# Masked block of the attention probabilities left out, and a later finish of the differential norms

## Chip, cores and metric

The kernel runs on one core of one Trainium2 chip. The metric is the device time of one execution in microseconds (us), the median of three runs. Engines are named as in the profile: PE is TensorE's matmul, PEld its weight load, DVE is VectorE, ACT is ScalarE, POOL is GpSimd, SP is SyncE.

## What is computed

The reference is a decoder of four layers on 512 tokens of width 1024, all in float32. The first block has a layer with a short convolution and a layer with sparse attention (compressed, selected and window branches of 12 heads); both also attend to a memory. The second block has a layer of multi-head latent attention (8 heads) and one of differential attention (8 heads); each layer ends in a squared-ReLU MLP. What the change touches is causal attention:

```python
def _causal_probs(q_blk, k, q_start, scale):
    s = jnp.einsum('bqhd,bkhd->bhqk', q_blk, k).astype(jnp.float32) * scale
    s = jnp.where(k_idx[None, :] <= q_idx[:, None], s, -jnp.inf)
    return jax.nn.softmax(s, axis=-1)
...
        p1 = _causal_probs(q_blk[..., 0, :], k1, start, scale)
        p2 = _causal_probs(q_blk[..., 1, :], k2, start, scale)
        a = p1 - lam * p2
        return jnp.einsum('bhqk,bkhd->bqhd', a.astype(v.dtype), v)
    o = _rmsnorm(o, subln) * (1.0 - lambda_init)
```

A query never sees a later key, so of any two tiles of 128 queries and the two tiles of 128 keys at the same place, the block (earlier queries, later keys) of the probabilities is zero.

## The kernel before

Nearly every product is kept exact by a split: a float32 matrix is written as a high part (dtype float32r, `FR`) and a low part, `split` (L91 to L99, ACT writes the high part, DVE the low one), and three products high x high, high x low, low x high are added up in PSUM (`mm`, L91, so that all these matmuls stand under line L91 and are told apart by tile names). The instruction streams of the engines are put in order when the program is built: every instruction has a priority, its place in the code, and a planned time at which it is ready; each engine's queue is then run strictly in order on the chip. A tile gets a buffer when one of its tag is free. PSUM has eight banks, two each of the tags S, T, F and O.

Attention works in units, one for a head (in the sparse layer: a head and a branch) and a half of the queries, that is two query tiles. `pipeline` (L388) runs three stages of successive units a step or more apart:
- `first`: scores (tile `sp`, two bank S tiles), `soft_half` (L402: DVE subtracts the maximum, ACT takes the exponential into tile `z`), `scale_half` (L432, L435: POOL multiplies `z` by the reciprocal of the row sum). In differential attention `first` makes two score maps, and DVE adds them at L1436.
- `turned`: `probs_T` (L437) transposes the blocks of `z` on TensorE (tile `pT`, L451) and splits them into `pth` and `ptl`, both from the pool of six pairs that the split weights (`wh`, `wl`) come from as well. The block that is masked is not transposed; it is filled with zeros by a DVE memset (L441) and a POOL memset (L442).
- `second`: the product with the values, `av` (three products for a key tile, tiles `lo` in latent and `do` in differential attention) or `av_stack` (two products, tile `no`), each 256 queries wide, into a bank of tag O (`bankB`).

There are 48 units in the sparse layer (6 pairs of heads x 2 heads x 2 halves x 2 branches), 16 in latent and 16 in differential attention, 80 in all. Memory attention uses `av_stack` too, without a mask.

In differential attention `second` (L1443) goes on: ACT squares the product (L1452), TensorE sums the squares over the partitions (`ones`), DVE and POOL make the reciprocal root (`var` L127, `rstd` L129). What is left is the closure `third` (L1457): TensorE turns the root into a row in the other half of the same bank (L1459), ACT copies it (L1460), DVE multiplies (L1461), and a split writes `oT`. `third` of a unit is put into the list `pend` and called in the `second` of the next unit, after that unit's product with the values.

Steps are filled up with dense work (`fills`): in differential attention the query, key and value layer of later heads (tile `df`, steps 0 to 11) and half of the output layer (tile `wo`, one unit of 12 matmuls in steps 10 to 17). The head's transposes of its keys (tile `dkT`) take a bank of tag O as well.

Of the kernel before, what the change touches and what calls it, by code (L numbers as in the profile page):

```python
# [32 lines left out]
def model_kernel(ctx: ExitStack, tc: tile.TileContext, I, out, tap=lambda *a: None, stop=0):  # L33
# [67 lines left out]
    # ------------------------------------------------------------ constants  # L101
# [30 lines left out]
    # ------------------------------------------------------------ weights  # L132
# [24 lines left out]
    # ------------------------------------------------------------ dense layers  # L157
    def dense_a(nK, lhs, weights, chunks, evac, tail=4, ntok=MT, late=None, ahead=3, hook=None):
        """Token-major layer: activations stationary, weights moving; late() brings the last token tile."""
        nch = len(chunks)  # L160
        dst = {}

        def alloc(t):
            if t in dst:
                return
            if nch == 2:
                if t == 0:
                    rot["S"] = rot["T"] = 0
                dst[t] = list(bankST("acc")) if t < 3 else [bankB("acc"), bankB("acc")]
            else:  # L170
                dst[t] = [bankT("acc") if t % 2 else bankS("acc")]

        W = {}

        def step(k, t, cs=range(nch)):
            alloc(t)
            wh, wl = W[k]
            lh, ll = lhs(k, t)
            for a, b, st, sp in ((lh, wh, k == 0, False), (lh, wl, False, False), (ll, wh, False, k == nK - 1)):
                for c in cs:  # L180
                    c0, c1 = chunks[c]
                    mm(dst[t][c][:, :c1 - c0], a, b[:, c0:c1], st, sp)

        head = max(0, nK - tail)
        k0 = 0
        if late is not None:
            k0 = min(ahead, nK)
            for k in range(k0):
                W[k] = weights(k)
            for t in range(ntok):  # L190
                if t == 2:
                    late()
                for k in range(k0):
                    step(k, t)
        for k in range(k0, head):
            W[k] = weights(k)
            for t in range(ntok):
                step(k, t)
        k0 = max(k0, head)
        for k in range(k0, nK):  # L200
            W[k] = weights(k)
        if hook:
            hook()
        for t in range(ntok):
            if nch == 2 and t == ntok - 1:
                for c in range(2):
                    for k in range(k0, nK):
                        step(k, t, (c,))
            else:
                for k in range(k0, nK):  # L210
                    step(k, t)
            evac(t, [dst[t][c][:, :c1 - c0] for c, (c0, c1) in enumerate(chunks)])

    def dense_b(xh, xl, nK, nU, weights, late, early):
        """Feature-major layer: units of 256 features; weights(u, k0) gives 4 k tiles.  With late(), the first
        two units take tokens 0-255 before it and 256-511 after it.  Yields the unit's PSUM tile; with early, the
        next unit's weights are asked for before that."""
# [41 lines left out]
    # ------------------------------------------------------------ norms and transposes  # L259
# [24 lines left out]
    def next_xT(norm):  # L284
        """norm(t, ps) -> token-major tile.  The last tile's transposes are left to the next layer (box["late"])."""
        box = {}

        def after(t, ps):
            if t == 0:
                box["xT"] = new_xT()  # L290
            if t > 0:
                to_xT(box["xT"], t - 1, box["src"])
            src = box["src"] = norm(t, ps)
            if t == MT - 1:
                box["late"] = lambda: to_xT(box["xT"], t, src, True)

        return after, box
# [33 lines left out]
    def dup_heads(src):  # L331
        """[P, t, (2 heads, 64)] -> [P, t, head, twice, 64]."""
        d = w4("dup").rearrange("p (t h r d) -> p t h r d", t=MT, h=2, r=2)
        for r in range(2):
            nc.gpsimd.tensor_scalar(d[:, :, :, r, :], src.rearrange("p t (h d) -> p t h d", h=2), 1.0, 1.0,
                                    op0=OP.mult, op1=OP.mult)
        return d
# [6 lines left out]
    # ------------------------------------------------------------ parameter columns  # L344
# [28 lines left out]
    def stack(dst0, dst1, T, key):  # L373
        """T [(head0 d; head1 d), cols] -> [high; low] of each head, gains applied."""
# [12 lines left out]
    # ------------------------------------------------------------ attention pieces  # L387
    def pipeline(units, lags, extras=None, fills=None, started=0):  # L388
        """Step s issues stage i of unit s - lags[i]; extras, fills: {step: closures issued before, after}."""
# [12 lines left out]
    def soft_half(half, scores, bias, scale):  # L402
        """Query tiles 2*half, 2*half+1: exp(s - max) in z[:, b, :], reciprocal row sums."""
# [20 lines left out]
    def falling(v):  # L424
        """The columns of v in falling order."""
        n = v.shape[-1]
        return bass.AP(tensor=v.tensor, offset=v.offset + n - 1, ap=[list(v.ap[0]), [-1, n]])
# [9 lines left out]
    def probs_T(half, z):  # L437
        """-> key tile -> [keys, 256 queries], high and low parts.  The masked block leads the last pair of tiles."""
        h, l = pair("pt")
        o = half * 512  # L440
        nc.vector.memset(h[:, o:o + P].bitcast(FT), 0.0)  # L441
        nc.gpsimd.memset(l[:, o:o + P].bitcast(FT), 0.0)  # L442
        for a in range(half + 1):
            T = bankT("pT")
            skip = P if a == half else 0
            for c in range(2):
                kt = 2 * a + (1 - c if skip else c)
                for b in range(2):
                    c0 = c * 256 + b * P
                    if c0 >= skip:  # L450
                        nc.tensor.transpose(T[:, c0:c0 + P], z[:, b, kt * P:(kt + 1) * P], ident)  # L451
            cs = slice(a * 512 + skip, (a + 1) * 512)
            split(h[:, cs], l[:, cs], T[:, skip:])

        def tile_of(kt):
            k = (kt ^ 1 if kt // 2 == half else kt) * 256
            return h[:, k:k + 256], l[:, k:k + 256]

        return tile_of

    def av(o, vs, pt, nkt, first=True, last=True):
        for kt in range(nkt):
            vh, vl = vs(kt)
            ph, pl = pt(kt)
            mm(o, vh, ph, first and kt == 0, False)
            mm(o, vh, pl, False, False)
            mm(o, vl, ph, False, last and kt == nkt - 1)

    def av_stack(o, vs, pt, nkt, first=True, last=True):
        """vs(kt): [keys, (high | low) of 64 columns]; rows 0-63 and 64-127 of o add up to the product."""  # L470
        for kt in range(nkt):
            ph, pl = pt(kt)
            mm(o, vs(kt), ph, first and kt == 0, False)
            mm(o, vs(kt), pl, False, last and kt == nkt - 1)
# [7 lines left out]
    # ------------------------------------------------------------ memory attention  # L482
# [7 lines left out]
    def mem_kv(L, mT):  # L490
        """Emits the layer's key/value product; the returned closure finishes the keys."""
# [31 lines left out]
    def mem_attention(L, qm, ks, v, oT):  # L523
# [10 lines left out]
        for i in range(0, MT, 2):  # L534
            for a in range(2):
# [25 lines left out]
                def second(i=i, a=a, st=st):  # L561
# [10 lines left out]
                    for b in range(2):  # L572
                        ob = bankB("mo")[:, :256]
                        av_stack(ob, lambda kt: v[:, kt, 2 * a + b].rearrange("p s d -> p (s d)"), lambda kt: (h[:, b, kt], l[:, b, kt]), 2)
# [9 lines left out]
    def wrounds(src, ld, c0, n, key=None):  # L584
        """Blocks of k tiles of n columns, row gains applied when key is given."""
# [27 lines left out]
    def w_out_part(src, base, oT, ks, alpha=None):  # L613
        """Units that add k tiles ks of the output layer to the residual ahead of w_out."""
# [57 lines left out]
    # ------------------------------------------------------------ rotary tables  # L672
# [38 lines left out]
    def rope(dst, src, t, nh, nf, key):  # L711
        """dst, src: [P, nh, head width]; rotates the first 2*nf columns."""
# [13 lines left out]
    # ============================================================ first block, layer 0  # L726
# [5 lines left out]
    # ---- relative bias functions of the second layer  # L732
# [110 lines left out]
    # ============================================================ first block, layer 1  # L843
    # ---- keys, values, queries, gates
# [30 lines left out]
    # ---- compressed keys and values  # L875
# [78 lines left out]
    # ---- compressed, selected and window branches  # L954
# [181 lines left out]
    # ============================================================ second block  # L1136
# [16 lines left out]
    # ---- multi-head latent attention  # L1153
# [49 lines left out]
    def rope_q(g4):  # L1203
        """Rotated query parts of heads 4*g4 .. 4*g4 + 3, token-major."""
# [106 lines left out]
    # ---- differential attention  # L1311
# [18 lines left out]
    def diff_w(n, half):  # L1330
        """Half of the weights of part n % 3 of round n // 3."""
# [3 lines left out]
    def diff_round(r, bank):  # L1335
        """Dense units of heads 2*r, 2*r + 1: rotated queries and keys, split values, all token-major."""
# [64 lines left out]
    for h in range(8):  # L1401
# [17 lines left out]
        for half in range(2):  # L1419
# [23 lines left out]
            def second(h=h, half=half, st=st, ph=ph):  # L1443
# [5 lines left out]
                while pend:  # L1449
                    pend.pop()()  # L1450
# [19 lines left out]
    pend.pop()()  # L1470
# [59 lines left out]
```

## Time and profile before

| what | value |
|---|---|
| median of 3 runs | 2418.26 us (2415.67 to 2418.78) |
| span of the profiled execution | 2418.3 us |
| PE busy | 2362.6 us, 98% of the span |
| PEld, DVE, ACT, POOL busy | 2032.3, 1223.3, 969.4, 273.6 us |
| chain that ended last | PE 89%, DVE 4%, ACT 3%, POOL 2%, issue 1%, DMA 1% |

The span of the profiled execution is, to its last digit, the median of the runs, so that microseconds of the trace can be taken off the median as they are. The three attention stages lie at about 676 to 876 us (sparse), 1275 to 1410 us (latent) and 1785 to 2037 us (differential). The duration of a matmul in the trace contains its latency; in a stream the next one starts earlier, and the distance between two starts is what a matmul costs.

### The profile page before, as it was taken

Reading aid. Unit: us, or ns where it says so; the run is one execution under the profiler, and the core shown is the slowest. Engines: PE = TensorE matmul, PEld = TensorE weight load, DVE = VectorE, ACT = ScalarE, POOL = GpSimd, SP = SyncE. Lnnn points to the kernel's source line nnn. Section 1 sums busy time; section 2 is a strip of 40 time slices with the busy share of each in tenths; the row PEclk is TensorE's granted clock in tenths of the full one; section 3 lists DMA queues with packets and bytes.
Section 4 is the critical chain, followed back from the end, with each engine's and each line's share of the span. In section 5 each row is a group of like instructions: output and inputs, shape, how many; then the busy total and the mean of one; then the engine's idle time right before and its main releaser. Section 6 shows DMA issues by size and latency. Waiting matters only on the chain.

```text
span 2418.3 us, 32335 instructions
## 1 busy us (share of the span) xinstructions
PE 2362.6 (98%) x12735; PEld 2032.3 (84%) x12735; DVE 1223.3 (51%) x2248; ACT 969.4 (40%) x1749; POOL 273.6 (11%) x458
## 2 busy tenths in 40 slices
PE   8999999999988999999999999999999999999998
PEld 7878888888877888888888888888889997888886
DVE  5564333336678873333347773333356667433334
ACT  4353332225468853332225543222235555323222
POOL 0220000000345520000001100000011222000000
PEclk9999999999999999999999999999999999999999
DMA  6223322224211133222221133322221112332222
GB/s 199 88 75 122 105 89 86 96 96 139 67 36 36 45 102 105 89 87 96 96 84 47 63 113 105 105 79 96 96 90 53 63 62 79 122 105 79 96 96 70
DMA packets 149538, 214.90 MB, mean 89 GB/s; under 512 B 12570, under 2 KB 119389, under 8 KB 149386
## 3 DMA queue, kind: packets, MB, share of 16 engines
q1 hardware_dynamic: 148718, 212.54, 27.5%
q8 instruction: 100, 1.64, 0.3%
q14 instruction: 52, 0.43, 0.1%
q10 hardware_dynamic: 668, 0.30, 0.0%
HBM read 210.68 MB, written 2.13 MB: 88 GB/s over the span
## 4 chain that ended last, share of the span: by engine, by line
PE 89%; DVE 4%; ACT 3%; POOL 2%; issue 1%; DMA 1%; ACTq 0%; POOLq 0%; DVEq 0%
PE pus L91 17%; PE put L91 16%; PE acc L91 13%; PE accs L91 13%; PE acct L91 12%; PE df L91 5%; PE sp L91 3%; PE wo L91 2%; PE pT L451 2%; POOL z L435 1%; PE do L91 1%; POOL rstd L129 1%; PE no L91 1%; PE qks L91 1%; PE lo L91 1%
## 5 line engine op out<-in xcount | busy, mean ns | idle before, releaser
L96 DVE TENSOR_TENSOR wl<-raw,wh 128x1024 fp32r<-128x1024 f32 (+3 forms) x366 | 441.0, 1207 | 529.5 <-ACT wh L95 524.7
L95 ACT ACTIVATE wh<-raw 128x1024 fp32r<-128x1024 f32 (+3 forms) x366 | 378.1, 1038 | 559.5 <-PE acc L91 312.7
L129 POOL TENSOR_TENSOR rstd<-var,mhalf 128x1 f32<-128x1 f32 (+3 forms) x91 | 76.8, 844 | 1705.1 <-DVE var L127 1705.1
L91 PE MATMUL pus<-xTh,wh 128*128 128x512 f32 (+1 forms) x664 | 243.3, 367 | 1.9 <-ACT xTh L95 1.2
L91 PE MATMUL pus<-xTl,wh 128*128 128x512 f32 (+1 forms) x664 | 242.2, 365 | 0.0
L91 PE MATMUL pus<-xTh,wl 128*128 128x512 f32 (+1 forms) x664 | 241.9, 364 | 0.0
L91 PE MATMUL put<-xTl,wh 128*128 128x512 f32 (+1 forms) x664 | 241.6, 364 | 0.0
L91 PE MATMUL put<-xTh,wh 128*128 128x512 f32 (+1 forms) x664 | 241.5, 364 | 0.0
L91 PE MATMUL put<-xTh,wl 128*128 128x512 f32 (+1 forms) x664 | 241.4, 363 | 0.0
L96 DVE TENSOR_TENSOR rl<-r,rh 128x1024 fp32r<-128x1024 f32 x64 | 78.2, 1224 | 160.7 <-ACT rh L95 160.7
L91 PE MATMUL accs<-wh,rh 128*128 128x512 f32 x384 | 149.8, 390 | 0.9 <-ACT rh L95 0.9
L91 PE MATMUL acct<-wh,rh 128*128 128x512 f32 x384 | 149.8, 390 | 0.0
L91 PE MATMUL accs<-wl,rh 128*128 128x512 f32 x384 | 149.5, 389 | 0.0
L91 PE MATMUL accs<-wh,rl 128*128 128x512 f32 x384 | 149.3, 389 | 0.0
L91 PE MATMUL acct<-wl,rh 128*128 128x512 f32 x384 | 149.3, 389 | 0.0
L91 PE MATMUL acct<-wh,rl 128*128 128x512 f32 x384 | 149.1, 389 | 0.0
L658 DVE SCALAR_TENSOR_TENSOR r<-pus,rr 128x512 f32<-128x512 f32 x64 | 44.3, 692 | 203.6 <-ACT rr L657 203.6
L91 PEld LDWEIGHTS pus<-xTh,wh 128*128 128x128 f32 x664 | 125.9, 190 | 22.5 <-ACT xTh L95 2.4
L91 PEld LDWEIGHTS pus<-xTl,wh 128*128 128x128 f32 x664 | 126.1, 190 | 19.6 <-DVE xTl L96 0.2
L91 PEld LDWEIGHTS pus<-xTh,wl 128*128 128x128 f32 x664 | 125.7, 189 | 19.5
L91 PEld LDWEIGHTS put<-xTh,wl 128*128 128x128 f32 x664 | 125.4, 189 | 19.8
L91 PEld LDWEIGHTS put<-xTl,wh 128*128 128x128 f32 x664 | 125.4, 189 | 19.6
(443 smaller groups left out, 5120.6 us busy)
## 6 DMA issues: line engine op xcount, KB each, us to landing
raw<-in_w_up_dram SPq DMA_DIRECT2D x64, 512.0 KB, 3.6
raw<-in_w_down_dram SPq DMA_DIRECT2D x64, 512.0 KB, 3.5
raw<-in_ffn_w_up_dram SPq DMA_DIRECT2D x64, 512.0 KB, 4.1
raw<-in_ffn_w_down_dram SPq DMA_DIRECT2D x64, 512.0 KB, 3.5
raw<-in_diff_w_qkv_dram SPq DMA_DIRECT2D x24, 512.0 KB, 3.6
raw<-in_a_w_in_dram SPq DMA_DIRECT2D x20, 512.0 KB, 3.4
raw<-in_w_out_dram SPq DMA_DIRECT2D x16, 512.0 KB, 3.9
raw<-in_mem_w_kv_dram SPq DMA_DIRECT2D x8, 512.0 KB, 4.9
```

What stands on the lines that cost most here:

```text
L91: return nc.tensor.matmul(o, a, b, start=start, stop=stop, skip_group_check=True)
L95: nc.scalar.activation(h, src, AF.Copy)
L96: nc.vector.tensor_sub(l, src, h.bitcast(FT))
L129: nc.gpsimd.tensor_tensor(r, v, mhalf[:np_, :w], op=OP.pow)
L435: nc.gpsimd.tensor_scalar(z[:, b, :nq], z[:, b, :nq], rc[:, b:b + 1], sc[b], op0=OP.mult, op1=OP.mult)
L451: nc.tensor.transpose(T[:, c0:c0 + P], z[:, b, kt * P:(kt + 1) * P], ident)
L658: nc.vector.scalar_tensor_tensor(r2[u // 4][:, (2 * u) % 8 + m, :], ps[m], 0.0, rr[:, m, :], op0=OP.max, op1=OP.mult)
```

## The change

Four edits. `probs_T` no longer fills the masked block: the transposed blocks stand at the front of the bank, and the last key tile has 128 columns in place of 256. The products with that tile are 128 columns wide and add to the second half of the output; they are issued before the last of the wide products (`av_seq`). Memory attention keeps full width under a name of its own (`av_full`). In differential attention `third` of a unit is called in the `second` of the unit after the next, and after the last unit two of them are left. The rest of the diff takes away comments.

```diff
     def probs_T(half, z):
         h, l = pair("pt")
-        o = half * 512
-        nc.vector.memset(h[:, o:o + P].bitcast(FT), 0.0)
-        nc.gpsimd.memset(l[:, o:o + P].bitcast(FT), 0.0)
         for a in range(half + 1):
             T = bankT("pT")
-            skip = P if a == half else 0
+            n = 512 if a < half else 384
             for c in range(2):
-                kt = 2 * a + (1 - c if skip else c)
                 for b in range(2):
-                    c0 = c * 256 + b * P
-                    if c0 >= skip:
+                    if a < half or b >= c:
+                        c0 = c * 256 + b * P - (P if a == half and c else 0)
+                        kt = 2 * a + c
                         nc.tensor.transpose(T[:, c0:c0 + P], z[:, b, kt * P:(kt + 1) * P], ident)
-            cs = slice(a * 512 + skip, (a + 1) * 512)
-            split(h[:, cs], l[:, cs], T[:, skip:])
+            split(h[:, a * 512:a * 512 + n], l[:, a * 512:a * 512 + n], T[:, :n])

         def tile_of(kt):
-            k = (kt ^ 1 if kt // 2 == half else kt) * 256
-            return h[:, k:k + 256], l[:, k:k + 256]
+            k = slice(kt * 256, kt * 256 + (P if kt == 2 * half + 1 else 256))
+            return h[:, k], l[:, k]

+    def av_seq(o, prods, nkt, first, last):
+        wide = [p for kt in range(nkt - 1) for p in prods(kt)]
+        seq = [(o, *p) for p in wide[:-1]] + [(o[:, P:], *p) for p in prods(nkt - 1)] + [(o, *wide[-1])]
+        for n, (oo, w, m) in enumerate(seq):
+            mm(oo, w, m, first and n == 0, last and n == len(seq) - 1)
+
     def av(o, vs, pt, nkt, first=True, last=True):
-        for kt in range(nkt):
-            vh, vl = vs(kt)
-            ph, pl = pt(kt)
-            mm(o, vh, ph, first and kt == 0, False)
-            mm(o, vh, pl, False, False)
-            mm(o, vl, ph, False, last and kt == nkt - 1)
+        def prods(kt):
+            (vh, vl), (ph, pl) = vs(kt), pt(kt)
+            return [(vh, ph), (vh, pl), (vl, ph)]
+
+        av_seq(o, prods, nkt, first, last)

     def av_stack(o, vs, pt, nkt, first=True, last=True):
+        av_seq(o, lambda kt: [(vs(kt), p) for p in pt(kt)], nkt, first, last)
...
                 av(ob[:, :256], lambda kt: (v[:, 0, kt, hc], v[:, 1, kt, hc]), pt, 2 * half + 2)
-                while pend:
-                    pend.pop()()
+                while len(pend) > 1:
+                    pend.pop(0)()
...
     pipeline(units, (0, 1, 2), extras, fills)
-    pend.pop()()
+    while pend:
+        pend.pop(0)()
```

## Rows read from the trace of the kernel before

**Rows 1.** Page, part 1: busy us (share of the span) and instructions.
```profile
PE 2362.6 (98%) x12735; PEld 2032.3 (84%) x12735; DVE 1223.3 (51%) x2248; ACT 969.4 (40%) x1749; POOL 273.6 (11%) x458
```
**Rows 2.** Busy us by stretch: length, PE, PEld, DVE, ACT, POOL, PEclk, DMA share, GB/s.
```profile
676.00:716.00 40.00, 33.44 (x250) 30.90 (x248) 29.25 (x87) 21.18 (x57) 19.82 (x33) 0.96 0.06 21
...
sum 200.00, PE 182.20 PEld 160.99 DVE 167.58 ACT 153.16 POOL 112.41; mean PE 36.44 PEld 32.20 DVE 33.52 ACT 30.63 POOL 22.48
...
sum 135.00, PE 133.10 PEld 119.42 DVE 101.27 ACT 77.35 POOL 22.41; mean PE 26.62 PEld 23.89 DVE 20.25 ACT 15.47 POOL 4.48
...
1915.00:1980.00 65.00, 65.00 (x506) 62.12 (x505) 45.69 (x117) 38.51 (x95) 14.24 (x20) 1.00 0.20 66
1980.00:2037.00 57.00, 52.30 (x311) 43.92 (x311) 40.65 (x105) 31.08 (x76) 17.38 (x24) 0.97 0.22 73
```
**Rows 3.** Who waited for whom, TensorE, whole program: us in total, times, longest.
```profile
PE do L1459 <- POOL rstd L129: 4.7, 4, 2.6
PE pT L451 <- POOL z L435: 4.4, 11, 0.7
```
**Rows 4.** Tile grs: duration ns min/median/max, first and last start, form (plain float32 product).
```profile
L91 PE MATMUL grs<-oh x2: 1007/1030/1054, 6.0 to 6.8; 33*12 33x512 f32 x2
```
**Rows 5.** Timeline of TensorE: start us, us, engine, line, tiles, form, count.
```profile
676.14 1.49 PE L91 MATMUL sc<-kvn 128*128 128x32 f32 x12
...
705.46 0.28 PE L91 MATMUL no<-ptl,kvn 128*128 128x256 f32 x1
...
705.82 0.28 PE L91 MATMUL no<-kvn,vk 128*128 128x256 f32 x1
705.94 0.18 PE L91 MATMUL sc<-kvn,nq 128*128 128x32 f32 x1
```
**Rows 6.** The lines of the zero fills and of the transposes: duration ns min/median/max.
```profile
L441 DVE MEMSET pth<- x80: 165/165/165, 696.7 to 2009.4; 128x128 f32 x80
...
L442 POOL MEMSET ptl<- x80: 196/205/217, 694.9 to 2007.9; 128x128 f32 x80
...
L451 PE MATMUL pT<-ident,z x400: 270/272/421, 695.2 to 2028.8; 128*128 128x128 f32 x134
```
**Rows 7.** Timeline of the last steps of differential attention, all engines.
```profile
2004.89 0.39 PE L91 MATMUL wo<-wh,oTl 128*128 128x512 f32 x1
...
2007.18 0.75 DVE L1436 SCALAR_TENSOR_TENSOR z<-z,rc 128x512 f32<-128x512 f32 x1 [0.51 <-POOL z L435]
...
2007.88 0.69 PE L1459 MATMUL do<-ident,rstd 128*128 128x128 f32 x2 [2.60 <-POOL rstd L129]
...
2009.02 0.42 DVE L1461 TENSOR_TENSOR dn<-do,dn 128x256 f32<-128x256 f32 x1 [0.53 <-ACT dn L1460]
...
2011.35 0.27 PE L451 MATMUL pT<-ident,z 128*128 128x128 f32 x1
...
2024.77 0.39 PE L91 MATMUL wo<-wh,oTh 128*128 128x512 f32 x1
...
2026.07 0.75 DVE L1436 SCALAR_TENSOR_TENSOR z<-z,rc 128x512 f32<-128x512 f32 x1 [0.51 <-POOL z L435]
...
2026.76 0.43 PE L1459 MATMUL do<-ident,rstd 128*128 128x128 f32 x2 [1.60 <-POOL rstd L129]
...
2028.30 0.82 PE L451 MATMUL pT<-ident,z 128*128 128x128 f32 x6
```
**Rows 8.** Busy us by stretch, just behind the longest of these waits.
```profile
2007.60:2010.90 3.30, 3.02 (x9) 2.43 (x10) 1.62 (x8) 1.25 (x5) 0.53 (x3) 0.51 0.22 87
```
**Rows 9.** Busy us of TensorE with tile wo alone behind the two waits: length, PE, PEclk, DMA share, GB/s.
```profile
2007.88:2011.40 3.52, 3.18 (x7) 0.55 0.12 47
2026.76:2028.30 1.54, 1.35 (x5) 1.00 0.41 143
```
**Rows 10.** Tile do: duration ns min/median/max, first and last start.
```profile
L1459 PE MATMUL do<-ident,rstd x32: 270/272/473, 1864.7 to 2036.5; 128*128 128x128 f32 x32
...
L1461 DVE TENSOR_TENSOR dn<-do,dn x16: 394/424/425, 1868.9 to 2037.2; 128x256 f32<-128x256 f32 x16
```

More of the change, by code (lines that the diff above doesn't have):

```diff
@@ L469, in av_stack, with av_full @@
     def av_stack(o, vs, pt, nkt, first=True, last=True):
+        av_seq(o, lambda kt: [(vs(kt), p) for p in pt(kt)], nkt, first, last)
+    def av_full(o, vs, pt, nkt):
         for kt in range(nkt):
             ph, pl = pt(kt)
-            mm(o, vs(kt), ph, first and kt == 0, False)
-            mm(o, vs(kt), pl, False, last and kt == nkt - 1)
+            mm(o, vs(kt), ph, kt == 0, False)
+            mm(o, vs(kt), pl, False, kt == nkt - 1)
     def unstack(h, l, o, tmp):
@@ L573, in second @@
                         ob = bankB("mo")[:, :256]
-                        av_stack(ob, lambda kt: v[:, kt, 2 * a + b].rearrange("p s d -> p (s d)"), lambda kt: (h[:, b, kt], l[:, b, kt]), 2)
+                        av_full(ob, lambda kt: v[:, kt, 2 * a + b].rearrange("p s d -> p (s d)"), lambda kt: (h[:, b, kt], l[:, b, kt]), 2)
                         p0 = slice(b * 64, b * 64 + 64)
```

## Prediction

> **What bounds the kernel now.** I read the page first: TensorE is busy 98% of the span, no other engine over half [rows 1]. What doesn't shorten TensorE's stream or one of its stalls is then worth nothing. Next, the busy table by stretch, since the change touches three stages alone. In latent attention TensorE is busy 133.1 of 135 us, and in the body of differential attention 65.0 of 65 [rows 2]; there only less matmul time counts. Two places have stalls. In sparse attention TensorE is busy 182.2 of 200 us; 6.6 of the 17.8 idle us lie in the first 40, in which DVE is busy 29.3 [rows 2]. In the last 57 us of differential attention it is busy 52.3 [rows 2]. Then the waits: the dearest one of the attention stages is the transpose of the norm, `do` L1459, for POOL's `rstd`: 4.7 us in four waits, 2.6 the longest; the transposes of the probabilities wait 4.4 us for POOL's scaling, but in eleven small pieces [rows 3].
>
> **Narrow products.** 48 sparse units have two products with the last key tile, 32 others have three: 96 + 96 = 192 products go from 256 to 128 columns. No row shows a float32r product of 128 columns, so I bound it. A stream of 256-column products starts one each 0.120 us (705.46 to 705.94 is four of them) [rows 5]. The same stream with 32 columns: twelve in 1.49 us, the last of which lasts 0.26, so (1.49 - 0.26)/11 = 0.112 us [rows 5]. An eighth of the columns saves 8 ns; something that doesn't depend on the columns sets 0.112, and each of these products has its own weight load of 128 columns. A product of 128 columns must lie between these two: 0 to 8 ns less each. One 32-column product that found its weights loaded lasts 0.18 where the 256-column ones last 0.28 [rows 5]: 0.10 us for 224 columns, 0.45 ns a column, so 128 columns stream in 57 ns and fit under 0.112. I take 8 ns: 192 x 8 = 1.5 us of TensorE time. The 96 of the saturated stages count in full (0.77 us), the 96 of sparse attention by half, as TensorE is not full there (33.4 of 40 us in its first stretch [rows 2]): **1.15 us**. That they are issued before the last wide product adds no wait, because both parts of `pth` and `ptl` come out of the same split. The number of transposes stays 400 [rows 6], and so do the splits' columns (384 and 512).
>
> The Trainium skill, TensorE: Matmul & The Clock Gate, section "Back-to-back issue gap", gives a distance of N/2.4 + 2.5 ns, which would halve such a product; its section "LDWEIGHTS (loading the stationary operand)" gives columns/1.2, an estimate of 107 ns for 128. By the first rule alone the 192 products would save about 10 us, by the second next to nothing, and the 0.112 us of the 32-column stream agrees with the second.
>
> **Zero fills.** 80 fills of 0.165 us leave DVE and 80 of 0.205 us leave POOL [rows 6], 13.2 and 16.4 us. The 32 of latent and differential attention lie beside a full TensorE and are costed at nothing. The 48 of sparse attention are 7.9 of DVE's 167.6 busy us (4.7%) and 9.8 of POOL's 112.4 (8.7%) [rows 2]. The loop there is DVE, ACT, POOL, TensorE, ACT, DVE, TensorE, and a stall lasts as long as those queues are. If TensorE's idle 17.8 us shrink by both shares, that is 17.8 x 0.134 = 2.4 us. Upper bound: each of the 48 units stalls TensorE and loses a DVE fill from its path, 7.9 us. Lower bound: the order planned for the queues is a new one and costs as much as that gain, -2.4 us. I take **2.0**, since the idle time is spread over many small waits and isn't due to the fills themselves.
>
> The fill was also what first took the pair of buffers. Without it the pair is taken when ACT writes `pth`, after the transposes, and weight loads from the same pool may get there first; that is part of the -2.4.
>
> **Norms one unit later.** TensorE's queue is in order. At 2005.28 it had finished `wo`, and the next in its queue was the transpose of a norm, which waited 2.60 us for `rstd`, itself queued on POOL behind the scaling of `z`; `wo` products that needed nothing stood behind it [rows 7]. A second place is 2025.16 to 2026.76, 1.60 us [rows 7]. With `third` one unit later, its place in the order is behind one more step of fill (12 `wo` products), so that the ready products come first. At the first place seven of them ran after the wait [rows 9] (1.6 us at the 0.23 us of full clock), and the transposes of the next probabilities went on until 2011.6; the probabilities themselves were ready at 2007.93 [rows 7]. So TensorE has work until 2006.9 and has the probabilities from 2007.9: the 2.6 us come off whole, as the transposes move from 2011.35 to about 2008. At the second place five of them ran after the wait [rows 9], 1.1 us, and the probabilities, ready at 2026.82, were transposed at 2028.3 [rows 7]: 1.1 of 1.6 us. Together **3.7 us**. Bounds: upwards all 4.7 us of rstd waits [rows 3], and the clock: in the 3.3 us behind the longest wait, in which TensorE had been idle for 2.6 us, the granted clock was 0.51, the 1.2 GHz level [rows 8]; without that wait half of it, 1.6 us, may come back, so 6.3. Downwards: below nothing, see the bank. What is late next is POOL's scaling of `z`, which the fill covers as far as it reaches.
>
> Moved with `third` are its ACT copy, DVE product and the split; no DMA and nothing on SP's queue. They wait in ACT's and DVE's queues less than before, because their transposes are later. After the last unit two are left in place of one; the first has its `rstd` long since, and the output layer has the first half of the tokens to work on: no cost.
>
> **The sum.** 1.15 + 2.0 + 3.7 = 6.85 us off 2418.3: **2411.5 us** (-0.28%). Own range of this case 2405 to 2416.
>
> **Rivals.**
>
> *The bank held longer (slower).* A unit's bank of tag O is now kept until the unit after the next, and there are two such banks. The product with the values of that later unit, and each head's `dkT`, must then wait until the pending `third` has been transposed, copied and multiplied. That takes 1.56 us at the first place above (2007.88 to 2009.44) [rows 7], and 4.6 us for the first unit (1864.7 to 1868.9 and 0.4) [rows 10]. While `df` fills the steps this is covered. In the last six steps only 12 `wo` products are left for each (2.7 us). If 1.3 us is uncovered in each of the six and the gain of the norms is lost, 7.8 - 3.15: 2423.0, range 2420 to 2430. It decides from where the release, queues included, exceeds the step's own fill. For it: ACT and DVE are also the busiest in these steps (DVE 40.7 of 57 us [rows 2]). Against it: the order is planned with free banks known, so that the transposes are put before the products that need the bank. 16%.
>
> *Nothing but the saturated part.* The stalls move: the `wo` products that fill a wait now are missing a microsecond later, and the sparse stage's new order has other waits. Left are 0.77 us and little else: 2417.0, range 2414 to 2420. For it: DVE is busy over 70% of both places [rows 2]. 26%.
>
> *Narrow products at a slower rate.* Plain float32 products stream at (1030 - 165)/512 = 1.69 ns a column (165 ns being the latency, 280 less 256 x 0.45) [rows 4, 5]. If float32r fell to that below 256 columns, 128 columns take 216 ns, 96 more than now: 192 x 96 = 18.4 us, less 5.7: 2431.0. Against it stands the 32-column product, at 0.45 ns a column. 4%.
>
> *No floor by the weights.* If products of 128 columns ran at 57 ns and a little, they would save some 58 ns each, 11 us: 2418.3 - 11.1 - 5.7 = 2401.5. The 0.112 us stream speaks against it. 2%. It is what the gap rule of the Trainium skill's page TensorE: Matmul & The Clock Gate would make of it.
>
> **How the numbers follow.** Forecast 52%; bank 16%; nothing 26%; slow rate 4%; no floor 2%. A measurement tells about 0.2%, 4.8 us, from no change: faster is below 2413.4, slower above 2423.1. Of the forecast four fifths lie below 2413.4 (0.41), with the no-floor case 0.43. Slower: 0.11 of the bank, the slow rate, and 0.02 of stalls that grow: 0.17. The rest is 0.40. The range 2405 to 2423 takes in the forecast's bounds, the case of nothing and the better half of the bank's; outside stay the slow rate, no floor and the worse half, some 15 to 18%.
>
> **What would show it.** Right: line L1459 gone from TensorE's waits, no half clock near 2008, the last 57 us of differential attention shorter by some 3 us, `lo` and `do` streams with three starts 0.112 apart in each unit, idle TensorE time of sparse attention 2 us less. Wrong: waits of `do` or `dkT` for DVE L1461 (bank), narrow products 0.2 us apart (rate), or the same idle time under other names (nothing). Latent attention is a control: it should be shorter by 0.4 us and no more.

## The result, and the profile after

The changed kernel takes 2431.15 us (2430.62 to 2431.75, four runs) beside 2418.52 us for the kernel before: the ratio is 1.0051, 95% interval 1.0037 to 1.0065. It is 12.6 us slower, where 6.85 us less were forecast. The profiled execution spans 2430.0 us, 11.7 more than the one before.

The page, part 1, busy time, share and instructions of each engine:

```profile
PE 2370.0 (98%) x12735; PEld 2030.7 (84%) x12735; DVE 1216.4 (50%) x2168; ACT 970.7 (40%) x1749; POOL 254.6 (10%) x378
```

Against [rows 1], 80 instructions are gone from DVE and 80 from POOL, and POOL's busy time fell by 19.0 us. TensorE has as many instructions as before and is busy 7.4 us longer. So the change did what it says, and the time came in as stalls and broken streams of TensorE.

To find the place I cut both traces at the same work: sparse attention with its output layer (first `no` to the first product of the next MLP layer), latent attention (last `latTt` or `latTs` to the last `lo`), differential attention with its output layer (first `df` to the next MLP layer). Busy time by stretch of the kernel before (length; busy us and count of PE, PEld, DVE, ACT, POOL; PEclk, DMA share, GB/s):

```profile
699.10:893.10 194.00, 177.76 (x1150) 154.78 (x1151) 165.31 (x493) 154.27 (x403) 103.33 (x197) 0.98 0.14 43
1284.70:1405.60 120.90, 120.22 (x759) 107.69 (x758) 91.71 (x237) 69.54 (x166) 20.21 (x48) 1.00 0.22 67
1786.60:2057.80 271.20, 264.18 (x1928) 245.54 (x1927) 183.72 (x451) 142.32 (x333) 60.18 (x85) 0.99 0.22 69
```

The same three stages of the changed kernel:

```profile
700.30:894.20 193.90, 178.03 (x1148) 151.39 (x1148) 157.60 (x443) 151.96 (x401) 92.48 (x150) 1.00 0.14 43
1285.80:1416.90 131.10, 124.00 (x758) 107.73 (x758) 88.86 (x219) 70.56 (x166) 18.41 (x32) 1.00 0.18 54
1798.10:2069.70 271.60, 266.31 (x1927) 246.18 (x1927) 184.28 (x434) 143.54 (x333) 53.71 (x69) 0.99 0.22 69
```

Latent attention, the control of the prediction, grew from 120.9 to 131.1 us at the full clock of 1.00: 10.2 of the 11.7 us. Differential attention is 0.4 us longer and sparse attention 0.1 shorter; the remaining 1.2 us lie ahead of the first `no` (700.3 beside 699.1). In latent attention TensorE's idle time grew by 6.4 us (120.9 less 120.2 before, 131.1 less 124.0 now) and its busy time by 3.8.

The five dearest of TensorE's waits of the changed kernel in latent attention (waiter <- releaser: us in total, times, longest):

```profile
PE qks L91 <- DVE ptl L96: 1.3, 1, 1.3
PE pT L448 <- POOL z L435: 1.0, 3, 0.5
PE pT L448 <- DVE vq L385: 0.9, 1, 0.9
PE lo L91 <- ACT pth L95: 0.9, 2, 0.6
PE lo L91 <- DVE ptl L96: 0.6, 2, 0.3
```

With the smaller ones they come to 6.8 us; in the kernel before, this stage had 0.7 us of such waits in all. Now TensorE waits for the splits of the probabilities (`pth`, `ptl`), which it did not wait for before. The first place shows how. Timeline of the kernel before, rows of four engines (start, us, engine, line, tiles; in brackets the idle time before, and its releaser):

```profile
1300.98 0.17 DVE L441 MEMSET pth<- 128x128 f32 x1
...
1303.41 0.62 ACT L95 ACTIVATE wh<-raw 128x512 fp32r<-128x512 f32 x1
...
1304.41 0.84 ACT L95 ACTIVATE wh<-raw 128x768 fp32r<-128x768 f32 x1
...
1305.60 0.49 PE L451 MATMUL pT<-ident,z 128*128 128x128 f32 x3
1305.84 0.36 PE L91 MATMUL acc<-wh,cTh 128*128 128x256 f32 x1
...
1306.12 0.49 ACT L95 ACTIVATE pth<-pT 128x384 fp32r<-128x384 f32 x1 [0.88 <-PE pT L451]
```

The same work of the changed kernel, which is some 1.1 us later there:

```profile
1306.73 0.62 ACT L416 ACTIVATE z<-z,mx 128x384 f32<-128x384 f32 x1 [1.23 <-DVE mx L413]
1306.74 0.49 PE L448 MATMUL pT<-ident,z 128*128 128x128 f32 x3
1307.34 0.48 ACT L95 ACTIVATE pth<-pT 128x384 fp32r<-128x384 f32 x1
1307.87 0.38 PE L91 MATMUL lo<-pth,vq 128*128 128x256 f32 x1 [0.64 <-ACT pth L95]
1308.42 1.36 ACT L95 ACTIVATE wh<-raw 128x512 fp32r<-128x512 f32 x2
1309.09 0.74 PE L91 MATMUL acc<-wh,cTh 128*128 128x256 f32 x4
```

Before, the zero fill wrote `pth` 4.6 us ahead of the transposes, and ACT split the two next weights (`wh`, 512 and 768 columns) ahead of them too. So dense products (`acc`) stood ready behind the transposes, and the splits of the probabilities ran under them. Now ACT idles 1.23 us and splits both weights after `pth` (the row of 1.36 us is the two of them, under the form of the first). TensorE has nothing dense to do, takes the product with the values right behind its own transposes, and waits for both splits.

### The profile page after: what moved, and what is told of

It is laid out like the page before. It is cut to its first block, busy times and chain, and to the rows that moved or that the text cites. A ratio compares the mean times of both kernels' runs of the same rounds, so it can differ in the third digit from the quotient of the medians.

```text
span 2430.0 us, 32191 instructions
## 1 busy us (share of the span) xinstructions
PE 2370.0 (98%) x12735; PEld 2030.7 (84%) x12735; DVE 1216.4 (50%) x2168; ACT 970.7 (40%) x1749; POOL 254.6 (10%) x378
## 4 chain that ended last, share of the span: by engine, by line
PE 86%; DVE 5%; ACT 4%; POOL 2%; issue 1%; DMA 1%; ACTq 0%; POOLq 0%; DVEq 0%; SPq 0%
PE pus L91 17%; PE put L91 16%; PE acc L91 12%; PE accs L91 12%; PE acct L91 12%; PE df L91 5%; PE wo L91 2%; PE sp L91 2%; PE pT L448 1%; ACT z L416 1%; PE do L91 1%; POOL rstd L129 1%; POOL z L435 1%; PE qks L91 1%; DVE wl L96 1%
```

## The experiments

All ratios are to the kernel before, measured beside each run on the same chip.

**One part at a time.** e1_norms is the kernel before with only

```
-                while pend:
-                    pend.pop()()
+                while len(pend) > 1:
+                    pend.pop(0)()
```

and the loop after the last unit; e2_probs is the changed kernel with this undone.

> The kernel before with one part of the change alone: the norms of differential attention finish one unit later; zero fills and 256-column products are as before. Theory order (the loss of the whole change sits in latent attention, whose queues were put in another order because of what was done to the probabilities): latent attention keeps its time, 121.1 us from the last latT transpose to the last lo product, and the differential stage gains what the prediction said, 3.7 us or a little less; time about 2415. Rival bank (the norms are worth nothing, or cost, because the O bank is held longer): the differential stage is the same or longer; time 2418 to 2423.

> The change without its last part: no zero fills and 128-column products, the norms finish as before. Theory order: the loss is all here, latent attention takes some 131 us from the last latT to the last lo in place of 121, time about 2430. Rival bank (norms carry part of the loss): 2424 or less.

e1_norms took 2417.11 us (before 2419.46), ratio 0.9991, 0.9982 to 1.0000; e2_probs 2435.29 us, ratio 1.0069, 1.0054 to 1.0084. So the late norms help a little, the bank is no cost, and the whole loss is in the probabilities. e2_probs is 5 us above what was expected of it: latent attention takes 131.2 us, as expected, but sparse attention took 197.6 in this execution (last section) and differential attention 273.7. Differential attention of e1_norms, busy time, and what is left of [rows 3] in its waits:

```profile
1786.20:2054.30 268.10, 263.85 (x1928) 244.66 (x1927) 182.89 (x450) 144.27 (x333) 54.22 (x85) 1.00 0.23 70
...
PE do L1459 <- POOL rstd L129: 0.6, 1, 0.6
```

The wait fell from 4.7 to 0.6 us, and the stage from 271.2 to 268.1.

**Fills or width.** e3_fill_narrow has the narrow products of e2_probs with both fills of 128 columns kept, on columns that nothing reads; e4_nofill_wide has no fills, and the product with the last key tile is 256 columns wide again (it reads the 128 columns ahead as well):

```
+        o = half * 512 + 384
+        nc.vector.memset(h[:, o:o + P].bitcast(FT), 0.0)
+        nc.gpsimd.memset(l[:, o:o + P].bitcast(FT), 0.0)
```

> 128-column products, but the two zero fills are kept: they now write the last 128 columns of the pair, which nothing reads. Norms as before. Theory pair (without the fill the pair of buffers is taken only after the transposes, and the plan of the queues in latent attention tips over): latent attention is back at about 121 us, time 2416 to 2419. Rival width (the planner prices a 128-column product differently, and this puts the queues in a worse order): latent attention stays at some 131 us, time about 2430.

> No zero fills, but products of 256 columns: the product with the last key tile takes in the 128 columns that stand before it in the pair, so that the first query tile of each half comes out as something else than the reference's; the amount of work is that of the kernel before. Norms as before. Theory pair: latent attention stays at some 131 us, time about 2430. Rival width: latent attention is back at about 121 us, time about 2417. If neither or both of the two kernels lose, the order is sensitive to any such change and neither part is the cause by itself.

e3_fill_narrow: 2422.06 us, 1.0011 (1.0002 to 1.0021). e4_nofill_wide: 2427.39 us, 1.0038 (1.0025 to 1.0051). Latent attention of e3_fill_narrow, then of e4_nofill_wide:

```profile
1289.00:1409.80 120.80, 119.94 (x759) 107.30 (x758) 91.77 (x237) 69.46 (x166) 20.78 (x48) 1.00 0.23 67
```

```profile
1285.10:1412.60 127.50, 123.28 (x759) 108.06 (x759) 87.96 (x219) 70.56 (x166) 18.43 (x32) 1.00 0.19 56
```

With the fills there is no loss in latent attention, at either width; without them 6.6 us at the old width and 10.2 at the new one. The removed fills, the smallest edit of the four, are the cause of the loss in latent attention; its size depends on the width as well. The total of e3_fill_narrow was expected at 2416 to 2419 and isn't: sparse attention took 196.9 us in this execution, 2.9 more than in the kernel before.

**Their time, or that they are there.** e5_tiny is the changed kernel with fills of 2 columns in place of 128; e6_dve has the fill of 128 columns of the high part alone.

> The changed kernel with two fills put back, but of 2 columns each, on columns that nothing reads (DVE for the high part, POOL for the low one); the products stay narrow and the norms late. Theory (order): what the fills did was to take the pair of buffers before the transposes, which sets the planned order of TensorE and of the splits; their duration has no part in it. Latent attention (last latT to last lo) is back from 131.1 to about 121 us, the total near 2431.2 - 10.3 = 2421, and down to 2419 if the late norms count as in e1_norms. Rival (duration): the planner needs an instruction of 0.2 us there; with tiny ones latent attention stays at 128 to 131 us and the total above 2427.

> The changed kernel with the fill of the high part alone put back (DVE, 128 columns that nothing reads), none on POOL. In the planned order about half of the latent units then have the product with the values behind dense work again, and the first and two of the last units have it directly behind their own transposes. Theory (order): latent attention between the two, 123 to 127 us, total 2423 to 2427. Rival (either fill is enough, since each takes the pair): latent 121 us, total 2419 to 2421. Rival (POOL's fill is the one that matters): latent 129 to 131 us, total 2429 to 2432.

e5_tiny: 2416.26 us (before 2419.01), ratio 0.9988, 0.9978 to 0.9998. Its three stages:

```profile
701.50:894.20 192.70, 177.69 (x1148) 151.07 (x1147) 158.78 (x489) 152.16 (x401) 96.24 (x195) 1.00 0.15 44
1285.80:1406.60 120.80, 119.95 (x759) 107.32 (x759) 89.75 (x237) 69.50 (x166) 19.08 (x48) 1.00 0.23 67
1787.70:2055.20 267.50, 263.99 (x1928) 244.40 (x1927) 181.61 (x450) 143.92 (x333) 52.22 (x85) 1.00 0.23 70
```

The duration has no part in it: two columns bring latent attention back whole. The total is 3 to 5 us below what was expected, because differential attention is 4.1 us shorter too (267.5 beside 271.6). e6_dve: 2429.66 us, ratio 1.0046 (1.0031 to 1.0061), with latent attention in between:

```profile
1288.70:1414.10 125.40, 122.51 (x759) 107.24 (x758) 90.28 (x236) 70.78 (x166) 20.49 (x32) 1.00 0.19 56
```

Its 125.4 us lies in the middle of the expected 123 to 127. So each of the two tiles counts, that of the high part for ACT's splits and that of the low part for DVE's: from the last `latTt` on, ACT splits five weights ahead of the first `pth`, as in the kernel before (three in the changed kernel), but DVE only three ahead of the first `ptl`, as in the changed kernel (four before). The total was expected at 2423 to 2427 and isn't: differential attention (272.8 us) got nothing back, and sparse attention was long in this execution (198.6 us).

**Order on TensorE, or the weights.** The product with the values directly behind its own transposes looked like the cause. e7_order leaves the fills out and ties TensorE's order in latent attention at this one point: a unit's first product with the values comes behind the last transpose of the next unit's probabilities:

```
+            i = mm(oo, w, m, first and n == 0, last and n == len(seq) - 1)
+            if n == 0 and turn_last.get("on"):
+                order(i, turn_last["i"])
```

> The changed kernel without any fill; in latent attention alone TensorE's order is tied: the first product with the values of a unit may not stand before the last transpose of the next unit's probabilities. The pairs are taken as late as in the changed kernel. Theory (order on TensorE is what costs): latent attention back from 131.1 to 121 to 124 us, total 2421 to 2425. Rival (the pair: the weights of the values are split later on ACT and DVE because nothing reserves the pair, so the dense products are late whatever TensorE's order): latent attention stays at 127 to 131 us, the waits move from lo to acc, total 2427 to 2432.

2432.01 us, ratio 1.0052 (1.0037 to 1.0067): the theory of TensorE's order fell (121 to 124 us of latent attention were expected from it). Latent attention, its dearest waits, and the place of the timeline shown above:

```profile
1285.80:1417.30 131.50, 123.39 (x759) 107.27 (x758) 88.74 (x219) 70.67 (x166) 18.47 (x32) 1.00 0.18 54
...
PE acc L91 <- ACT wh L95: 1.9, 1, 1.9
...
PE qks L91 <- ACT wh L95: 1.2, 3, 0.7
...
1307.30 0.48 ACT L95 ACTIVATE pth<-pT 128x384 fp32r<-128x384 f32 x1
...
1308.38 1.35 ACT L95 ACTIVATE wh<-raw 128x512 fp32r<-128x512 f32 x2
...
1309.05 0.62 PE L91 MATMUL acc<-wh,cTh 128*128 128x256 f32 x3 [1.86 <-ACT wh L95]
```

The stage is as long as without the tie. The same time now stands under other names: the dense products wait 1.86 us for `wh`, which ACT still splits behind `pth`. The changed order of TensorE was a symptom; the weights are late.

**Why the weights are late.** In the changed kernel's timeline above, ACT idles ahead of `z` and not ahead of the split of `wh` at 1308.42: the trace shows no wait of that split, it stands behind `pth` in the order planned for ACT. The weights concerned are asked for in the step after the one that asks for the pair of these probabilities, and both come from the same six pairs. If the plan hands out pairs in the order of the code, at a tile's first write, then a pair whose first write is the split after the transposes holds back every later weight. e9_early puts this to the test without any fill. It asks for the weights of latent attention (load and split) one step earlier, ahead of those transposes, and changes nothing else in the code:

```
+            at(4 * hp - 6 - 1, lambda hp=hp: rope_w(hp // 2))
             at(4 * hp - 6, lambda hp=hp: rope_q(hp // 2))
+        at(4 * hp - 2 - 1, values_w)
         at(4 * hp - 2, values)
...
+            at(4 * hp + 2 * hh - 3 - 1, head_w)
             at(4 * hp + 2 * hh - 3, head)
```

> The changed kernel without any fill, also in order and products as it is; only the requests for the weights of latent attention (load and split of the query, value and rotary weights) stand one step earlier in the code, ahead of the transposes that they stood behind; the products with them stay where they were. Theory (turn): buffers of a tag are handed out in code order, at a tile's first write. With no fill the pair of the probabilities is first written by ACT's split behind the transposes, and weights asked for later in the code wait for that in ACT's and DVE's queues, so the dense products on TensorE are late. Then latent attention comes back from 131.1 to 121 to 122 us with no fill at all, the total to 2420 to 2422. Rival (the fills gave something else, time or a place in the queues of DVE and POOL): latent attention stays at 128 to 131 us, total 2428 or more.

2421.88 us (before 2418.85), ratio 1.0017 (1.0007 to 1.0027). Latent attention, and the same place of the timeline:

```profile
1286.40:1408.40 122.00, 119.92 (x759) 107.21 (x758) 88.45 (x218) 69.60 (x165) 18.89 (x32) 1.00 0.19 56
...
1303.55 0.84 ACT L95 ACTIVATE wh<-raw 128x768 fp32r<-128x768 f32 x1
...
1306.20 0.49 PE L448 MATMUL pT<-ident,z 128*128 128x128 f32 x3
1306.45 0.36 PE L91 MATMUL acc<-wh,cTh 128*128 128x256 f32 x1
```

9.1 of the 10.2 us are back with no fill in the kernel, and the weights are split ahead of the transposes again. So it is shown that the weights are late where they are asked for behind a pair that is first written late, and on time where either that write comes early (e5_tiny, with the weights at their old place in the code) or they are asked for ahead of the pair. That the plan hands out pairs strictly in code order is the rule that I infer from the two. e9_early doesn't prove it by itself, since an earlier place in the code is also a higher priority for the loads and splits.

**Where the rest lies.** e8_second is e1_norms with narrow products and fills of 2 columns in latent and differential attention alone (sparse attention as before). e10_latfill is the changed kernel with fills of 2 columns in latent attention alone:

```
+        if take:
+            o = half * 512 + 384
+            nc.vector.memset(h[:, o:o + 2].bitcast(FT), 0.0)
+            nc.gpsimd.memset(l[:, o:o + 2].bitcast(FT), 0.0)
```

> Sparse attention as in the kernel before (full fills, 256-column products); in latent and differential attention narrow products with fills of 2 columns on unused columns; norms late. Theory (order): the three stages keep the order of the kernel before, so 0.8 us of narrow products and 2.4 us of norms come off 2418.5: 2415 to 2417, and the stretch up to sparse attention stays at 78.6 and sparse attention at 193.9 us. Rival (every change of the plan costs 1 to 3 us somewhere, as sparse attention did in e3_fill_narrow): 2418 to 2422.

> The changed kernel with the fills of 2 columns of e5_tiny in latent attention alone; sparse and differential attention without fills. Theory (turn): latent attention 121 us, total 2431.2 - 10.3 = 2421; what then still lies between it and e5_tiny (2416.3) is the fills' share in the other two stages: differential attention to the next MLP layer 271 to 272 us here, 267.5 there. Rival (what is lost in latent attention is only carried over from sparse attention): latent attention stays above 127 us, total above 2427.

e8_second: 2416.45 us, ratio 0.9990 (0.9981 to 1.0000). e10_latfill: 2420.48 us, ratio 1.0009 (0.9999 to 1.0018), as expected 10.7 below the changed kernel. Its latent and differential attention:

```profile
1286.40:1407.10 120.70, 119.85 (x758) 107.20 (x757) 89.73 (x237) 69.45 (x166) 19.08 (x48) 1.00 0.22 67
1788.30:2060.20 271.90, 266.87 (x1927) 245.98 (x1926) 184.04 (x433) 143.43 (x332) 53.70 (x69) 0.99 0.22 69
```

So differential attention is 4.4 us longer as well when its pairs are taken late (271.9 beside 267.5 in e5_tiny), which in the changed kernel hid the gain of the norms. A part of this has a name. The changed kernel's dearest wait in the last steps, what is left there of [rows 3], and the stretch behind the first of the two:

```profile
PE dqTs L342 <- POOL dup L335: 1.4, 1, 1.4
...
PE do L1464 <- POOL rstd L129: 0.2, 1, 0.2
...
2010.00:2014.00 4.00, 3.67 (x18) 3.52 (x19) 2.13 (x4) 1.95 (x4) 0.95 (x2) 0.63 0.42 131
```

The next head's queries, copied by POOL, now come 1.4 us late (no such wait stands in the kernel before, 0.4 us in e1_norms), and in the 4 us behind that, after TensorE had stood idle, the granted clock is 0.63, so most of them at the 1.2 GHz level. In e5_tiny the wait is 0.6 us and no stretch of this stage is below full clock in its rows. The clock did not fall each time. e9_early has no fills in differential attention either, the same order on every engine there and the same 1.4 us wait, but full clock:

```profile
1789.80:2059.80 270.00, 265.07 (x1928) 244.50 (x1927) 184.16 (x434) 143.54 (x333) 53.74 (x69) 1.00 0.22 70
```

So of the 4.4 us some 1.9 (271.9 to 270.0) went with the lower clock of these executions, and 2.5 are left without it; 0.8 of those are the longer wait, and the rest I did not follow. Nor did I settle why the loss in latent attention without fills is 3.6 us larger with narrow products (131.1 beside 127.5): the plan of the queues is another one in each, and no experiment here separates its steps.

The best kernels are e5_tiny and e8_second, at 2416.3 and 2416.5 us, with e1_norms at 2417.1 no further off than the measurement tells. The gain over the kernel before is 0.1%, and all three intervals end at or just below no change.

## Why the prediction was wrong, point by point

**Zero fills: the step that failed.** "The 32 of latent and differential attention lie beside a full TensorE and are costed at nothing." The duration of the fills was rightly worth nothing there, but the fill was also the first write of a pair, and without it latent attention lost 10.2 us and differential attention 2.5 to 4.4. The prediction named this ("weight loads from the same pool may get there first") and then made two errors. It had the direction the wrong way round: the weights don't get there first, they queue behind the pair that is taken late. And it put the effect into a lower bound of 2.4 us, worked out from the idle time of sparse attention. It belonged to the stages in which TensorE is full, since there TensorE is full only because split weights are always ready. The trace of before had the row for it: `pth` was first written at 1300.98, 4.6 us before its transposes, and two weights were split in between. The price of losing that cover could have been taken from the splits that may move behind the transposes. At the 0.62 us of the shorter `wh` row above, one for each of the 16 units of latent attention is 10 us for ACT alone: an estimate, four times the 2.4 us. It is made afterwards, with a count that no run checks, so that it lies near the 10.2 us is luck.

**Zero fills of sparse attention.** 2.0 us were forecast. Between e8_second, with full fills and wide products there, and e5_tiny, with fills of 2 columns and narrow products, the totals differ by 0.2 us. The stage is 2.3 us shorter (195.0 to 192.7), but the first `no` stands 2.2 us later in e5_tiny (701.5 beside 699.3), so that both end it at the same time, 894.3 and 894.2. Nothing of the 2.0 us shows. The stage in e8_second, to set beside that of e5_tiny above:

```profile
699.30:894.30 195.00, 179.33 (x1150) 156.04 (x1151) 165.45 (x493) 154.36 (x403) 102.80 (x197) 0.97 0.14 43
```

**Narrow products.** 1.15 us were forecast, at 112 to 120 ns from start to start. Timeline of TensorE, one short unit of latent attention: first its first product and what follows the unit in the kernel before, then the whole unit in e5_tiny:

```profile
1315.43 0.36 PE L91 MATMUL lo<-pth,vq 128*128 128x256 f32 x1
...
1316.22 0.39 PE L91 MATMUL qks<-cTh,wh 128*128 128x512 f32 x1
```

```profile
1316.57 0.36 PE L91 MATMUL lo<-pth,vq 128*128 128x256 f32 x1
1316.77 0.28 PE L91 MATMUL lo<-ptl,vq 128*128 128x256 f32 x1
1316.89 0.22 PE L91 MATMUL lo<-pth,vq 128*128 128x128 f32 x1
1316.95 0.27 PE L91 MATMUL lo<-ptl,vq 128*128 128x128 f32 x1
1317.06 0.44 PE L91 MATMUL lo<-pth,vq 128*128 128x128 f32 x2
1317.34 0.40 PE L91 MATMUL qks<-cTh,wh 128*128 128x512 f32 x1
```

The unit takes 0.77 us in place of 0.79, and the forecast of 8 ns for each of three products is 0.024. So the sum held, but not its distances (0.112 for all three were forecast): the second narrow product starts 0.06 us after the first, with the same tile of the values as its weights, the third 0.11 later, and the two products of the last row take 0.28 together, where 0.24 would be two full steps. Most of what the first product saves is lost again behind the last one. What sets the 0.06 isn't shown: the trace has a weight load for each of these products (144 for 144 `lo` products). In the kernel before it has one at 705.83 too, for the 32-column product of 0.18 us that the prediction took for one that found its weights loaded. In the stages the term can't be told from nothing. Where the pairs are taken in time, latent attention is 0.1 us shorter (120.8 beside 120.9), and differential attention took 267.5 us in e5_tiny and 268.2 in e8_second, which have the same order there, beside 268.1 of e1_norms. The total of the changed kernel, 2431, is by chance the number of the rival with the slow rate; these rows show that it is not its mechanism. On the gap rule of the Trainium skill, TensorE: Matmul & The Clock Gate, section "Back-to-back issue gap": the section gives the rule for a single product by itself, and the rows agree with it (56 ns for 128 columns) for that one distance of 0.06 us alone.

**Norms one unit later.** The wait of `do` for `rstd` went as forecast, from 4.7 to 0.2 us in the changed kernel and 0.6 in e1_norms. The term of 3.7 us was a little too large: e1_norms gains 3.1 us in differential attention and 2.35 in total (2419.46 to 2417.11; by its interval 0 to 4.4). The stage's granted clock rose from 0.99 to 1.00 with it, so a part of the 3.1 us is the clock, which the prediction had as an upper bound only, and the waits gave back less than the term says. The bank held longer cost nothing. In the changed kernel the gain was eaten by the late pairs of the same stage, and in the profiled execution by the lower clock behind them.

**The rivals.** None of the four was what happened. The nearest, "the stalls move", had no price for a stage that had no stalls.

**Latent attention as a control** was the best line of the forecast: it should have been 0.4 us shorter, was 10.2 us longer, and showed at once that the fills were more than their time.

## What to carry to other kernels

Before a write is removed because its data aren't needed, ask what else it does in the plan: the first write takes the buffer, and whatever asks for one of the same tag later in the code may have to wait for that. A stage with TensorE full is not safe ground where an edit is free; it is where the cover must be named, and where losing it costs most. If the write can go but the claim must stay, write two columns of it, or ask for the weights one step earlier.

## What the runs showed of the hardware that was not expected

Sparse attention differs between executions by more than some of the effects looked for. The changed kernel and e2_probs have the same order on every engine up to differential attention, yet the stage took 193.9 us in the one and 197.6 in the other. e7_order, e9_early and e10_latfill have that order in this stage too and took 193.6 to 194.0, so the long one is one of five. Busy time by stretch of the changed kernel, then of e2_probs, at the same work:

```profile
740.30:760.30 20.00, 17.73 (x128) 15.10 (x126) 16.15 (x54) 16.93 (x48) 10.85 (x17) 1.00 0.05 15
```

```profile
740.50:760.50 20.00, 18.46 (x113) 16.26 (x111) 14.70 (x47) 15.36 (x42) 8.92 (x14) 0.83 0.00 1
```

The granted clock was 1.00 in the one and 0.83 in the other, which did fewer products in the same 20 us (113 for 128). In this stage, where TensorE stalls often, a difference of 2 or 3 us between two profiled executions is no proof of a difference between the kernels.
